# Out rows in two places, nine begun strips, two-bank scores and the Hyena beside five heads in a two-layer hybrid step

## The chip, the cores and the metric

The kernel runs on one NeuronCore of a Trainium2 chip. Five engines work side by side, each through its own queue in order: PE (TensorE, the matrix multiplier), DVE (VectorE), ACT (ScalarE), POOL (GpSimd) and SP (SyncE, which here only starts DMA transfers). They wait for one another through semaphores. Matmul results land in PSUM, which has eight banks of 128 partitions by 512 fp32 numbers; everything else works on SBUF. The metric is the device time of one execution in microseconds, as the median of several.

## What is computed

One inference step of a two-layer backbone on 128 context tokens and 512 latent tokens (T = 640 tokens, D = 1024 channels). Each layer is a half-step SwiGLU, a mixer and a second half-step SwiGLU, each with an RMSNorm before it and a shift, a scale and a gate that depend on the conditioning vector. Layer 0's mixer runs RWKV-7 and a gated DeltaNet side by side, layer 1's runs latent attention (MLA) and an order-2 Hyena convolution. Cut to what the change touches:

```python
def swiglu(x, w_gu, w_down):
    g, u = jnp.split(x @ w_gu, 2, axis=-1)
    return (jax.nn.silu(g) * u) @ w_down          # F = 2816

def pre(x, g, m, j):
    return rmsnorm(x, g) * (1.0 + m[:, :, 3 * j + 1]) + m[:, :, 3 * j]

def rwkv7_mix(p, S0, mu, ...):
    p = p + mu * (centred_shift(p) - p)           # 0.5 * (previous + next token)
    r, k, v, wd, ad, gd = jnp.split(p, A_SPLITS, axis=-1)
    ...

def conv3(p, w):
    prev, nxt = neighbours(p)
    return w[0] * prev + w[1] * p + w[2] * nxt
```

The attention has 8 heads with 64 + 32 query and key channels and 64 value channels. Context tokens see the 128 context tokens, latent tokens see 128 cached tokens and the 512 latent ones, 640 keys, through an ordinary softmax. The Hyena takes 12 projections of 128 channels through conv3 and then two long convolutions, which are done as products with cosine and sine tables.

## The kernel before

Activations lie with channels on partitions: x as two halves (c = 0, 1) of 320 tokens, each 128 x 8 x 320. Products are done to fp32 precision by splitting each operand into a high part and a low part (hh and hl for the normed input, wh and wl for weights) and adding three matmuls. The split of a weight costs an ACT cast (wh) and a subtraction (wl) on DVE or POOL.

**The feed-forwards** (`ffn`, four times: ffn01, ffn02, ffn11, ffn12). The 22 strips of 128 hidden channels stand in five groups (FGROUPS: 5, 4, 4, 4, 5 strips). A strip is a Strassen-Winograd product: seven products of 12 matmuls over quarters of the input, 84 matmuls of 320 columns. Two of the seven need only the first token half. `first(f)` does these two ahead for the strips of group 0 (NE = 5): a *begun strip*, 24 matmuls, whose results wait in the tiles u2 (named u) and s1 (named s). Meanwhile `quarters` makes the sums that the other five products need: r0a and r0b are hi + lo of the first half (L601, on POOL, in the tiles hidh and hidl), then the second half is normed into r1a, r1b, and their differences are split into the tiles b0 to b5 and the second half's hh and hl (L605, on DVE). `strip(f)` then does the remaining products; the sums of weights S come from POOL (L684). After each group the down projection of its hidden strips is added into x (L550). The norm before an ffn is part of the tail of the stage before it (`branch`), so an ffn opens with its begun strips, while the norm of the second half is still being made. With `self.bg` (ffn01 and ffn02 still fetch modulation weights in the background) the strips carry further items beside them; in ffn11 and ffn12 `self.bg` is empty.

**The start.** In block one of the program the Hyena's filters are computed in PSUM banks of two kinds, four "mm" and four "mx". Then `banks(mm=8)` closes that pool and opens eight "mm" banks for ffn01.

**in_proj0** makes 32 rows of projections for layer 0's mixer. Each is a strip of 48 matmuls, copied into a padded tile pp, taken through a token shift (`shift`, 15 rows) or a three-tap convolution (`conv`, 16 rows, four heads of four; one in four only through SiLU) or stored as it is (`gate`) in a tile o, and written to the DRAM tensor pd (320 KB a row), from which the recurrences read it. `shift` adds the neighbours on POOL (nb, L878), scales on ACT (L881) and combines on DVE (L882). `self.t` keeps the number of buffers that was given at a tag's first use in its pool: `shift(0, ...)` comes first and asks for "o" without a number, so that o has one buffer for the whole pool.

**mixers1.** `latents` makes the query, key and value latents. `heads` is a generator over eight heads: `project` makes q and k, `softmax` the scores of 128 queries against 640 keys in two banks of 320, `values` transposes the probabilities pr into PT (L1779) and multiplies by V. `hyena_in` is a generator over the 12 strips of the Hyena's input, `hyena` over its convolutions. Four heads run with three strips each, then four heads with three Hyena steps each.

What sets the order: the code above records instructions in Python order, and the tile framework's scheduler then places them on the engines' queues by a timeline that it models itself, so instructions of neighbouring stages mix. Pools are released tile by tile.

## Time and profile before

| | us |
|---|---|
| three runs | 3175.32, 3182.38, 3186.39 |
| median | 3182.38 |
| the profiled execution | 3187.08 |
| its span | 3185.1 |
| mean granted clock of PE | 0.957 |

The profile is of one execution, with times from the start of its span. A group of the profile stands by its line: L287 is every matmul of the helper `mm`, so tiles tell more than lines there. A busy PE is not a PE at its peak: in the openings of stages the granted clock (1.00 is full speed) drops, and a matmul of 320 columns takes longer. In brackets behind an instruction stands how long its engine sat idle before it and what it was released by; `DMA pd<-o` as a releaser is the writing of a row o to DRAM. Where the stages lie: the filters to about 88 us, ffn01 from there, in_proj0 and the recurrences from 575 to 1303, ffn11 from 1838, the latents of layer 1 up to 2366, heads and Hyena to 2661, ffn12 from 2721.

### The profile page before, as it was taken

To read this page: it belongs to the slowest core of one execution; us is meant where nothing else is said; L and a number is where in the kernel's file an instruction comes from. 1 tells how busy PE (TensorE), PEld (TensorE's weight loads), DVE (VectorE), ACT (ScalarE), POOL (GpSimd) and SP (SyncE) were. 2 spreads that over 40 slices of the span, in tenths; PEclk is the share of its full clock that TensorE was granted. 3 is DMA by queue.
4 is the path that set the end of the run, shared out by engine and by line. 5 is a ranking of instruction groups with operands and counts; after the bars stand their busy time and mean duration, and the time that the engine had idled before them with its cause. 6 is when DMAs were issued, how large, how long until landed. Compare 5 with 4: busy or idle time off the path is not lost.

```text
span 3185.1 us, 56006 instructions
## 1 busy us (share of the span) xinstructions
PE 2958.5 (93%) x21505; PEld 2671.5 (84%) x21505; DVE 2267.1 (71%) x4011; ACT 1355.0 (43%) x2846; POOL 1200.8 (38%) x1114
## 2 busy tenths in 40 slices
PE   7799999998988998889999979999989989899998
PEld 2689999987865676879999979999979748899998
DVE  5956667668769666695666797777766786977777
ACT  3423334566365555442333453333545424433333
POOL 1733335225545220263333474444310021744442
PEclk9999999998888989889999989999999989999999
DMA  7465542455564332445553222222321215222222
GB/s 273 137 209 164 177 137 72 166 157 170 139 151 112 93 86 81 161 146 181 163 180 116 82 93 87 84 86 83 122 62 58 91 47 181 67 90 86 80 83 83
DMA packets 277587, 385.36 MB, mean 121 GB/s; under 512 B 128704, under 2 KB 161120, under 8 KB 275400
## 3 DMA queue, kind: packets, MB, share of 16 engines
q1 hardware_dynamic: 277160, 381.13, 38.3%
q8 instruction: 169, 2.77, 0.4%
q14 instruction: 98, 0.80, 0.1%
q0 software_dynamic: 160, 0.66, 0.0%
HBM read 330.29 MB, written 51.42 MB: 120 GB/s over the span
## 4 chain that ended last, share of the span: by engine, by line
PE 54%; DVE 10%; ACT 4%; DMA 4%; POOL 3%; issue 3%; SPq 1%; DVEq 0%; ACTq 0%; POOLq 0%
PE ps L287 52%; DMA wr<-in_wd_dram 2%; DVE wl L655 1%; POOL S L684 1%; DMA wr<-in_wo_dram 1%; DVE nx L539 1%; DVE wl L471 1%; POOL X L826 0%; POOL wl L655 0%; POOL inv L824 0%; PE ps L1778 0%; DMA pd<-o 0%; DVE nacc L514 0%; DVE b L605 0%; ACT wh L470 0%
## 5 line engine op out<-in xcount | busy, mean ns | idle before, releaser
L287 PE MATMUL ps<-hh,wh 128*128 128x320 f32 x2208 | 698.6, 318 | 17.8 <-DVE g L1901 7.1
L287 PE MATMUL ps<-hl,wh 128*128 128x320 f32 x2208 | 695.1, 316 | 5.4 <-POOL hl L546 2.7
L287 PE MATMUL ps<-hh,wl 128*128 128x320 f32 x2208 | 686.5, 315 | 5.3 <-DVE wl L471 4.2
L287 PE MATMUL ps<-b,wh 128*128 128x320 f32 x2112 | 480.5, 315 | 32.5 <-DVE b L605 17.2
L287 PEld LDWEIGHTS ps<-hh,wh 128*128 128x128 f32 x2208 | 422.4, 192 | 34.4 <-DVE g L1901 7.9
L287 PEld LDWEIGHTS ps<-hl,wh 128*128 128x128 f32 x2208 | 422.8, 192 | 9.7 <-POOL hl L546 3.9
L287 PEld LDWEIGHTS ps<-hh,wl 128*128 128x128 f32 x2208 | 420.3, 191 | 8.8 <-DVE wl L471 5.4
L287 PEld LDWEIGHTS ps<-b,wh 128*128 128x128 f32 x2112 | 360.7, 192 | 40.5 <-DVE b L605 19.4
L287 PE MATMUL ps<-hidl,wh 128*128 128x320 f32 x1248 | 383.7, 309 | 0.0
L287 PE MATMUL ps<-hidh,wh 128*128 128x320 f32 x1248 | 383.2, 312 | 0.0
L287 PE MATMUL ps<-hidh,wl 128*128 128x320 f32 x1248 | 381.7, 309 | 1.0 <-DVE wl L471 1.0
L550 DVE SCALAR_TENSOR_TENSOR x<-ps,mod,x 128x128 f32<-128x128 f32 (+2 forms) x528 | 212.4, 435 | 212.3 <-PE ps L287 211.7
L655 POOL TENSOR_TENSOR wl<-S,wh 128x512 fp32r<-128x512 f32 x176 | 260.5, 1480 | 264.8 <-ACT wh L654 261.6
L684 POOL TENSOR_TENSOR S<-wr,wu 128x512 f32<-128x512 f32 x88 | 125.2, 1423 | 600.9 <-DMA wr<-in_wgu_dram 394.9
L287 PE MATMUL ps<-b,wl 128*128 128x320 f32 x1056 | 330.6, 315 | 9.4 <-DVE wl L655 6.1
L470 ACT CAST wh<-wr 128x512 fp32r<-128x512 f32 (+2 forms) x210 | 157.7, 754 | 407.0 <-PE ps L287 318.0
L654 ACT CAST wh<-S 128x512 fp32r<-128x512 f32 (+1 forms) x264 | 201.0, 763 | 216.0 <-PE ps L287 163.7
L471 DVE TENSOR_TENSOR wl<-wr,wh 128x512 fp32r<-128x512 f32 (+2 forms) x210 | 186.5, 891 | 82.9 <-ACT wh L470 80.9
L287 PEld LDWEIGHTS ps<-hidh,wh 128*128 128x128 f32 x1248 | 232.9, 188 | 13.3 <-issue 7.4
L287 PEld LDWEIGHTS ps<-hidh,wl 128*128 128x128 f32 x1248 | 233.4, 188 | 1.5 <-DVE wl L471 1.5
L287 PEld LDWEIGHTS ps<-hidl,wh 128*128 128x128 f32 x1248 | 234.1, 188 | 0.0
L287 PEld LDWEIGHTS ps<-b,wl 128*128 128x128 f32 x1056 | 202.3, 192 | 13.8 <-DVE wl L655 8.5
(457 smaller groups left out, 5971.2 us busy)
## 6 DMA issues: line engine op xcount, KB each, us to landing
wmod<-in_wmod_dram SPq DMA_DIRECT2D x288, 256.0 KB
wr<-in_wgu_dram SPq DMA_DIRECT2D x108, 512.0 KB
wu<-in_wgu_dram SPq DMA_DIRECT2D x88, 512.0 KB
wr<-in_wd_dram SPq DMA_DIRECT2D x80, 320.0 KB
wr<-in_wd_dram SPq DMA_DIRECT2D x96, 256.0 KB
pd<-o SPq DMA_DIRECT2D x32, 320.0 KB
wr<-in_abg_dram SPq DMA_DIRECT2D x17, 512.0 KB
wr<-in_wo_dram SPq DMA_DIRECT2D x16, 512.0 KB
```

The source lines that it names most:

```text
L287: self.nc.tensor.matmul(out=out, lhsT=lhsT, rhs=rhs, start=start, stop=stop)
L470: nc.scalar.copy(out=wh, in_=w)
L471: nc.vector.tensor_sub(out=wl, in0=w, in1=wh.bitcast(F32))
L539: nc.vector.scalar_tensor_tensor(out=xn[:, a:b], in0=self.x[c][:, k, a:b], scalar=A, in1=r[:, a:b], op0=ALU.mult, op1=ALU.mult)
L550: self.nc.vector.scalar_tensor_tensor(out=self.x[c][:, d, a:b], in0=q[:, a:b], scalar=gate[:, cond, d:d + 1], in1=self.x[c][:, d, a:b], op ...
L654: nc.scalar.copy(out=hi, in_=r)
L655: eng.tensor_tensor(out=lo, in0=r, in1=f32(hi), op=ALU.subtract)
L684: G.tensor_tensor(out=out, in0=x, in1=y, op=op)
```

## The change

Six edits.

1. In `in_proj0` two places for "o" are allocated first in the pool, and every user asks for two. `shift` becomes a `conv3` with weights mu/2, 1 − mu, mu/2: two DVE passes per span in place of POOL's neighbour sum and one DVE pass.
2. `NE` becomes (5, 9): where no background is left (ffn11, ffn12), nine strips are begun, those of groups 0 and 1, and `quarters` is called behind the second begun strip instead of the first.
3. `softmax` takes both score banks as one tile: one reduction, one exponential with one sum, no joining of two maxima and two sums. From head 3 on, PT is copied by ACT.
4. `hyena_in` starts in the latents: one strip behind the query latent, two behind V. Three heads then run beside nine strips, and five heads beside the Hyena, two steps each.
5. The filters' banks stay open: block one goes on with "mm" and "mx" in turn, without closing the PSUM pool.
6. The two part sums of `quarters` (L601) go from POOL to DVE in all four ffns, with the second half's norm sum issued ahead of them.

```diff
--- before.py
+++ after.py
...
-NE = 5
+NE = (5, 9)
...
+NHS = 3
...
     def mm(self, out, lhsT, rhs, start=True, stop=True):
...
-    def ps(self, tag="mm"):
+    def ps(self, tag=None):
+        if tag is None:
+            tag, self.kinds = self.kinds[0], self.kinds[1:] + self.kinds[:1]
...
     def col(self, name, j=0, rows=slice(None)):
...
     def banks(self, **tags):
...
-        self.psum, self.tags = None, tags
+        self.psum, self.tags, self.kinds = None, tags, ["mm"]
...
-    def stat_end(self, c, tag="mm"):
+    def stat_end(self, c, tag=None):
...
-    def finish_norm(self, tag="mm", ks=range(KD), raw=None):
+    def finish_norm(self, tag=None, ks=range(KD), raw=None):
...
+        if self.nr[1] is None:
+            self.stat_end(1)
...
-            nc.gpsimd.tensor_tensor(out=r, in0=hi0[:, k].bitcast(F32), in1=lo0[:, k].bitcast(F32), op=ALU.add)
+            v.tensor_tensor(out=r, in0=hi0[:, k].bitcast(F32), in1=lo0[:, k].bitcast(F32), op=ALU.add)
...
         def split(to, r):
...
-        early = {}
+        early, ne = {}, NE[not self.bg]
...
         def first(f):
...
-            p1, s1 = tile("u2", NE), tile("s1", NE + 1)
+            p1, s1 = tile("u2", ne), tile("s1", ne + 1)
...
-                u, g0 = tile("u2", NE), tile("s1", NE + 1)
+                u, g0 = tile("u2", ne), tile("s1", ne + 1)
...
-                for f in range(NE):
+                for f in range(ne):
...
-                    if f == 0:
+                    if f == (ne > NE[0]):
...
+        out_ = lambda: self.t(ip, [P, T], "o", bufs=2)
+        for _ in range(2):
+            out_()
...
         def gate():
...
-            o = self.t(ip, [P, T], "o", bufs=2)
+            o = out_()
...
         def conv(hh, j):
...
-            o = self.t(ip, [P, T], "o", bufs=2)
+            o = out_()
...
-            nb = self.t(ip, [P, T + 1], "nb")
-            nc.gpsimd.tensor_tensor(out=nb, in0=p[:, 0:T + 1], in1=p[:, 2:T + 3], op=ALU.add)
-            o = self.t(ip, [P, T], "o")
-            for a, b, g in ((0, LP, 0), (LP, T, 1)):
-                nc.scalar.activation(out=o[:, a:b], in_=p[:, a + 1 + g:b + 1 + g], func=AF.Copy, scale=omu[:, mi:mi + 1])
-                nc.vector.scalar_tensor_tensor(out=o[:, a:b], in0=nb[:, a + g:b + g], scalar=hmu[:, mi:mi + 1],
-                                               in1=o[:, a:b], op0=ALU.mult, op1=ALU.add)
+            o = out_()
+            self.conv3(p, (hmu[:, mi:mi + 1], omu[:, mi:mi + 1], hmu[:, mi:mi + 1]), o)
...
-    def latents(self, h, first):
+    def latents(self, h, first, strips):
...
+        next(strips)
...
+        for _ in range(2):
+            next(strips)
...
     def heads(self, ap):
...
         def softmax(hh, qi):
...
-            ss = [self.ps("sc") for _ in keys]
-            mx = self.t(ap, [P, 2], "mxs", bufs=4)
-            sm = self.t(ap, [P, 2], "sms", bufs=4)
-            for i, (k0, n) in enumerate(keys):
-                self.mm(ss[i][:, :n], qt[hh][:96, P * qi:P * qi + P], kt[hh][:96, k0:k0 + n])
-                nc.vector.tensor_reduce(out=mx[:, i:i + 1], in_=ss[i][:, :n], axis=mybir.AxisListType.X, op=ALU.max)
-            if len(keys) > 1:
-                nc.vector.tensor_tensor(out=mx[:, :1], in0=mx[:, :1], in1=mx[:, 1:], op=ALU.max)
-            nc.vector.tensor_scalar(out=mx[:, :1], in0=mx[:, :1], scalar1=-scale, scalar2=None, op0=ALU.mult)
...
+            sc = self.psum.tile([P, 2, 512], F32, tag="sc", name=self.name("ps"), bufs=2)[:, :len(keys)]
+            n = keys[0][1]
+            mx = self.t(ap, [P, 1], "mxs", bufs=4)
+            sm = self.t(ap, [P, 1], "sms", bufs=4)
+            for i, (k0, _) in enumerate(keys):
+                self.mm(sc[:, i, :n], qt[hh][:96, P * qi:P * qi + P], kt[hh][:96, k0:k0 + n])
+            nc.vector.tensor_reduce(out=mx, in_=sc[:, :, :n], axis=mybir.AxisListType.XY, op=ALU.max)
+            nc.vector.tensor_scalar(out=mx, in0=mx, scalar1=-scale, scalar2=None, op0=ALU.mult)
...
-            for i, (k0, n) in enumerate(keys):
-                nc.scalar.activation(out=pr[:, i * H:i * H + n], in_=ss[i][:, :n], func=AF.Exp, scale=scale, bias=mx[:, :1],
-                                     accum_out=sm[:, i:i + 1])
-            if len(keys) > 1:
-                nc.vector.tensor_tensor(out=sm[:, :1], in0=sm[:, :1], in1=sm[:, 1:], op=ALU.add)
-            nc.vector.reciprocal(out=sm[:, :1], in_=sm[:, :1])
-            nc.vector.tensor_scalar(out=pr[:, :nk], in0=pr[:, :nk], scalar1=sm[:, :1], scalar2=None, op0=ALU.mult)
+            nc.scalar.activation(out=pr[:, :nk].rearrange("p (k n) -> p k n", n=n), in_=sc[:, :, :n], func=AF.Exp, scale=scale, bias=mx,
+                                 accum_out=sm)
+            nc.vector.reciprocal(out=sm, in_=sm)
+            nc.vector.tensor_scalar(out=pr[:, :nk], in0=pr[:, :nk], scalar1=sm, scalar2=None, op0=ALU.mult)
...
         def values(hh, qi):
...
-                nc.vector.tensor_copy(out=PT[hh][:, g:g + n, P * (qi - 1):P * qi],
-                                      in_=q[:, :P * n].rearrange("p (k t) -> p k t", k=n))
...
+                (nc.vector.tensor_copy if hh < NHS else nc.scalar.copy)(out=PT[hh][:, g:g + n, P * (qi - 1):P * qi],
+                                                                        in_=q[:, :P * n].rearrange("p (k t) -> p k t", k=n))
...
-                    q = self.ps("tr")
+                    q = self.ps("tr" if "tr" in self.tags else "mx")
...
-        self.banks(mm=8)
+        self.kinds = ["mm", "mx"]
...
-        self.latents(h, first)
...
+        sp = self.pool("strips", bufs=1, reuse_waits="tile")
...
+        strips = self.hyena_in(h, sp)
+        self.latents(h, first, strips)
...
-        sp = self.pool("strips", bufs=1, reuse_waits="tile")
-        heads, strips = self.heads(ap), self.hyena_in(h, sp)
-        for i in range(4):
+        heads = self.heads(ap)
+        for i in range(NHS):
...
-        for i in range(4, 8):
+        for i in range(NHS, 8):
...
-            for _ in range(3):
+            for _ in range(2):
...
```

What the scheduler makes of it, at three places. PE at the start of ffn01: nacc is the sum of squares of the second half, hmi and dfw belong to the last two filter products, and the row with hh, hl and wh is the first begun strip. Before:

```order
L287 MATMUL ps_553<-nacc_530,const_58 128x320
L287 MATMUL ps_499<-hmi_319,dfw_178 128x512 x2
L287 MATMUL ps_500<-hmi_319,dfw_178 128x512 x2
L287 MATMUL ps_647<-hh_581,wh_643 128x320
L287 MATMUL ps_647<-hl_582,wh_643 128x320
L287 MATMUL ps_647<-hh_581,wl_644 128x320
L287 MATMUL ps_647<-hh_581,wh_643 128x320
```

After, from the end of the first begun product on:

```order
L288 MATMUL ps_643<-hh_577,wl_640 128x320
L288 MATMUL ps_731<-hh_577,wh_727 128x320
L288 MATMUL ps_731<-hl_578,wh_727 128x320
L288 MATMUL ps_499<-hmi_319,dfw_178 128x512 x2
L288 MATMUL ps_500<-hmi_319,dfw_178 128x512 x2
L288 MATMUL ps_731<-hh_577,wl_728 128x320
L288 MATMUL ps_659<-hh_577,wh_639 128x320
L288 MATMUL ps_659<-hl_578,wh_639 128x320
```

The first begun product (ps_643) and the start of another strip's now stand ahead of the last two filter products.

DVE where ffn12's quarters are split. L673 is a begun strip's sum s, L655 the split of a weight (wr: of a begun strip), L605 the split pieces, L616 and L617 differences of quarters. Before, the end of that stretch:

```order
L673 TENSOR_TENSOR s_5240_29200<-ps_29202,u_5239_29199 128x320
L605 TENSOR_TENSOR b_5205_29057<-hidh_5200_29052,b_5204_29056 128x1280
L655 TENSOR_TENSOR wl_29274<-S_5256_29261,wh_29273 128x1024
L617 TENSOR_TENSOR hidh_5202_29054<-hidl_5203_29055,hidh_5202_29054 128x1280
L616 TENSOR_TENSOR hidh_5200_29052<-hidl_5203_29055,hidh_5200_29052 128x1280
L673 TENSOR_TENSOR s_5247_29236<-ps_29238,u_5246_29235 128x320
L605 TENSOR_TENSOR b_5207_29059<-hidh_5200_29052,b_5206_29058 128x1280
L605 TENSOR_TENSOR b_5209_29061<-hidh_5202_29054,b_5208_29060 128x1280
L605 TENSOR_TENSOR hl_29070<-hidl_5203_29055,hh_29069 128x1280
L605 TENSOR_TENSOR hl_29070<-hidl_5201_29053,hh_29069 128x1280
```

After (L678, L660, L610, L621 and L622 are the same lines there):

```order
L660 TENSOR_TENSOR wl_29173<-wr_29170,wh_29172 128x1024
L622 TENSOR_TENSOR hidh_5167_28936<-hidl_5168_28937,hidh_5167_28936 128x1280
L678 TENSOR_TENSOR s_5212_29118<-ps_29120,u_5211_29117 128x320
L621 TENSOR_TENSOR hidh_5165_28934<-hidl_5168_28937,hidh_5165_28934 128x1280
L660 TENSOR_TENSOR wl_29209<-wr_29206,wh_29208 128x1024
L678 TENSOR_TENSOR s_5219_29154<-ps_29156,u_5218_29153 128x320
L660 TENSOR_TENSOR wl_29258<-wu_29248,wh_29257 128x512
L610 TENSOR_TENSOR b_5172_28941<-hidh_5165_28934,b_5171_28940 128x1280
L610 TENSOR_TENSOR b_5174_28943<-hidh_5167_28936,b_5173_28942 128x1280
L610 TENSOR_TENSOR hl_28952<-hidl_5168_28937,hh_28951 128x1280
L678 TENSOR_TENSOR s_5226_29190<-ps_29192,u_5225_29189 128x320
```

Between the pieces b and hl now stand sums s of strips 5 to 8 and the splits of their weights wr.

DVE in a head: L1746 and L1755 (after) are the reduction of scores to a maximum, L1748 and L1755 (before) join two maxima and two sums, cv is a Hyena strip's convolution. Before, in an early head:

```order
L1746 TENSOR_REDUCE mxs_25835<-ps_25833 128x1
L1756 RECIPROCAL sms_25765<-sms_25765 128x1
L1748 TENSOR_TENSOR mxs_25810<-mxs_25810 128x1
L1757 TENSOR_SCALAR pr_25769<-pr_25769,sms_25765 128x128
L1749 TENSOR_SCALAR mxs_25810<-mxs_25810 128x1
L1755 TENSOR_TENSOR sms_25811<-sms_25811 128x1
L1756 RECIPROCAL sms_25811<-sms_25811 128x1
L1746 TENSOR_REDUCE mxs_25835<-ps_25834 128x1
L1757 TENSOR_SCALAR pr_25818<-pr_25818,sms_25811 128x640
L1748 TENSOR_TENSOR mxs_25835<-mxs_25835 128x1
L1749 TENSOR_SCALAR mxs_25835<-mxs_25835 128x1
```

After, also beside strips:

```order
L1755 TENSOR_REDUCE mxs_26796<-ps_26795 128x1
L1741 TENSOR_TENSOR q_26766<-ps_26781,rope_25342 32x320
L1742 TENSOR_TENSOR t_26767<-ps_26781,rope_25342 32x320
L1755 TENSOR_REDUCE mxs_26816<-ps_26815 128x1
L1756 TENSOR_SCALAR mxs_26796<-mxs_26796 128x1
L916 SCALAR_TENSOR_TENSOR cv_26752<-pp_4480_25643,cols_59,cv_26752 128x128
L916 SCALAR_TENSOR_TENSOR cv_26752<-pp_4480_25643,cols_59,cv_26752 128x512
L1756 TENSOR_SCALAR mxs_26816<-mxs_26816 128x1
L917 SCALAR_TENSOR_TENSOR cv_26752<-pp_4480_25643,cols_59,cv_26752 128x128
L1760 RECIPROCAL sms_26797<-sms_26797 128x1
L917 SCALAR_TENSOR_TENSOR cv_26752<-pp_4480_25643,cols_59,cv_26752 128x512
L1761 TENSOR_SCALAR pr_26802<-pr_26802,sms_26797 128x640
```

One reduction stands for two, and the two joining rows are gone.

More of the change, by code (lines that the diff above doesn't have):

```diff
@@ L2128, in mixers1 @@
         next(strips, None)
+        self.tc.swap_default_side()
         self.close(sp)
+        self.tc.swap_default_side()
         self.close_w()
```

2 lines of the change are left out of this document (added).

## The prediction

> **What bounds the kernel.** I read the page first: the span, the busy shares and the chain that ended last.
>
> ```profile
> span 3185.1 us, 56006 instructions
> PE 2958.5 (93%) x21505; PEld 2671.5 (84%) x21505; DVE 2267.1 (71%) x4011; ACT 1355.0 (43%) x2846; POOL 1200.8 (38%) x1114
> PE 54%; DVE 10%; ACT 4%; DMA 4%; POOL 3%; issue 3%; SPq 1%; DVEq 0%; ACTq 0%; POOLq 0%
> ```
>
> PE is busy 93% of the span, so 3185.1 − 2958.5 = 226.6 us are idle. Few products are taken out here, so nearly all that the change can win is in those 226.6 us and in the time after an idle stretch in which the granted clock is low. The second reading is therefore stage by stage, at the places that the diff touches: the busy time of each engine in windows. Columns are the stretch, then busy time (instructions) of PE, PEld, DVE, ACT, POOL, then the granted clock. These are the openings of ffn11 (two rows) and ffn12 (four rows).
>
> ```profile
> 1837.80:1849.30 11.50, 2.88 (x16) 1.88 (x14) 11.39 (x14) 7.47 (x17) 9.38 (x10) 0.74 0.39 141
> 1849.30:1891.00 41.70, 31.34 (x170) 28.95 (x171) 38.42 (x32) 21.70 (x33) 32.51 (x15) 0.83 0.26 86
> ...
> 2720.80:2739.40 18.60, 18.43 (x124) 17.87 (x122) 17.11 (x14) 11.30 (x19) 16.00 (x7) 1.00 0.36 121
> 2739.40:2763.30 23.90, 14.69 (x61) 13.05 (x62) 22.84 (x20) 11.80 (x18) 20.43 (x8) 0.79 0.18 60
> 2763.30:2804.50 41.20, 37.47 (x241) 35.10 (x240) 40.41 (x49) 14.87 (x27) 28.67 (x20) 1.00 0.24 81
> 2804.50:2880.00 75.50, 75.50 (x517) 75.50 (x516) 51.03 (x81) 25.87 (x43) 32.99 (x23) 1.00 0.29 88
> ```
>
> The five begun strips run at full rate (18.43 of 18.60). Then the quarters have to be made, and PE works 14.69 of 23.90 at a granted clock of 0.79 while DVE is 96% busy; until 2804.5 DVE is the bound (40.41 of 41.20). From there PE is. In ffn11 the hole is 11.50 − 2.88 = 8.6 us, then 10.4 us in the next row.
>
> **Nine begun strips (ffn11, ffn12).** The 124 matmuls of the first ffn12 row take 18.6 us, 0.150 each; a begun strip is 24 of them, 3.6 us, so four more are 14.4 us of PE per ffn that go ahead of the wait and no longer stand in group 1, where PE is the bound. If all of it fell into idle time each ffn would win 14.4. It will not, because DVE is full there. Prices of what the four strips and the part sums put on DVE:
>
> ```profile
> 2744.41 1.22 DVE L655 TENSOR_TENSOR wl<-S,wh 128x1024 fp32r<-128x1024 f32 x1
> 2745.55 1.48 DVE L617 TENSOR_TENSOR hidh<-hidl,hidh 128x1280 f32<-128x1280 f32 x1
> ...
> 2748.35 0.48 DVE L673 TENSOR_TENSOR s<-ps,u 128x320 f32<-128x320 f32 x1
> ```
>
> Four splits of 1.22, four sums of 0.48 and two part sums of 1.48 make 4.9 + 1.9 + 3.0 = 9.8 us. In ffn12 some 2 us fall into what DVE leaves free before 2739.4 and 2804.5 (1.5 + 1.1 + 0.8 = 3.4), and POOL, without its sums, stretches DVE less; I let group 0 end 6 us later. Group 1 (the last row begins with the products of group 0 and goes on with it) has room on DVE, 51.03 of 75.50, and each of its four begun strips needs 3.6 us less of PE, of which I count 2.75, as DVE can't quite keep that pace: −11. Net −5 in ffn12. ffn11 has the larger hole (8.6 + 10.4 = 19 us of idle PE in its rows against 0.2 + 9.2 + 3.7 = 13 in ffn12's first three), so −6. Bounds: −14.4 each if the holes swallow everything, +8 if DVE's 9.8 stretch further and group 1 gives back little. The four more weight loads of 512 KB lie where the DMA share is 0.36 or less.
>
> **Part sums on DVE (all four ffns).** Two adds leave POOL for DVE. What POOL's adds do to DVE is visible at the start of ffn01:
>
> ```profile
> 88.93 2.87 POOL L601 TENSOR_TENSOR hidl<-hh,hl 128x1280 f32<-128x1280 f32 x1
> ...
> 88.99 3.16 DVE L539 SCALAR_TENSOR_TENSOR nsq<-x,A,nacc 128x320 f32<-128x320 f32 x1
> 92.08 0.54 DVE L539 SCALAR_TENSOR_TENSOR nx<-x,A,nacc 128x320 f32<-128x320 f32 x1
> ```
>
> The same DVE form takes 3.16 beside the add and 0.54 just after. So one POOL add can cost DVE 2.6 us, and on DVE it costs 1.48. In ffn11 and ffn12 this is in the sum above. In ffn01 and ffn02 nothing else changes on DVE: I take −1 for both together, bounds −4 (the 2.6 saved twice, 1.48 paid twice, in each) and +6 (2.96 paid in each, nothing saved). [...]
>
> **The filters' PSUM banks kept in block one.** Before, ffn01's first product waits for the last bank of the filters.
>
> ```profile
> 94.06 0.68 DVE L1901 SCALAR_TENSOR_TENSOR g<-fa,ps 128x512 f32<-128x512 f32 x1
> ...
> 94.79 0.64 PE L287 MATMUL ps<-hh,wh 128*128 128x320 f32 x1 [7.09 <-DVE g L1901]
> 95.23 0.47 PE L287 MATMUL ps<-hl,wh 128*128 128x320 f32 x1
> ...
> 98.96 0.35 PE L287 MATMUL ps<-hh,wh 128*128 128x320 f32 x1
> ```
>
> That is 7.1 us of idle, and then 15 matmuls until 98.96 that take 4.2 us instead of 15 × 0.15 = 2.3: two more. Both can go, 9 us at most. But the work behind the begun strips waits for the quarters, whose DVE chain doesn't hang on these banks, so most of the 9 us will reappear as a wait for the pieces b. I count −3, bounds −9 and +3 (the products issued ahead delay the filters' own last ones, and with them the bank that DVE empties).
>
> **Out rows in two places (in_proj0).** The row "o" had one buffer, and each strip's activation waited until the row before was written out.
>
> ```profile
> L878 POOL TENSOR_TENSOR nb<-pp 128x641 f32<-128x641 f32 x15 | 27.3, 1818 | 65.5 <-issue 33.7 <-ACT pp L751 26.1 <-DVE o L882 5.6
> L882 DVE SCALAR_TENSOR_TENSOR o<-nb,hmu,o 128x512 f32<-128x512 f32 x15 | 13.1, 876 | 0.6 <-ACT o L881 0.6
> L913 DVE SCALAR_TENSOR_TENSOR o<-pp,cols,o 128x512 f32<-128x512 f32 x12 | 9.0, 754 | 0.2
> ...
>   DMA pd<-o: 65.6, 22
> ...
> 830.71 1.02 ACT L911 ACTIVATE o<-pp,cols 128x128 f32<-128x128 f32 x2 [11.93 <-DMA pd<-o]
> 898.49 0.77 ACT L864 ACTIVATE o<-ps 128x320 f32<-128x320 f32 x2 [3.27 <-DMA pd<-o]
> 899.72 2.50 PE L287 MATMUL ps<-wd,lora 128*128 128x320 f32 x4 [9.05 <-ACT w L1051]
> ...
> 775.00:825.00 50.00, 44.35 (x310) 41.03 (x311) 36.79 (x71) 18.82 (x43) 35.55 (x70) 0.83 0.60 155
> 825.00:875.00 50.00, 43.80 (x476) 42.31 (x475) 38.97 (x75) 17.38 (x36) 26.67 (x44) 0.86 0.46 140
> 875.00:925.00 50.00, 35.68 (x202) 27.25 (x200) 30.38 (x39) 27.34 (x69) 28.45 (x59) 0.83 0.55 143
> ```
>
> Engines stood 65.6 us, in 22 waits, for the write of o (tile view of o). Behind a waiting ACT queue the weight casts and the biases of the recurrence, and at 899.7 PE has been idle 9.05 us for one of them. PE's idle time in the three windows is 26.2 us, the clock another 150 − (0.83 + 0.86 + 0.83) × 50 = 24; together 50 us is the ceiling. Against it, DVE gets a second pass per span: 15 × (0.754 + about 0.35, the 128x128 form being about half) = 16.5 us, while POOL loses 27.3. SP's queue keeps its order of blocked writes and weight loads, so some of the waits stay. I take somewhat under a quarter of the 50: −11; bounds −26 (all the idle time) and +16 (DVE's second passes on the path, no wait gone).
>
> **Two-bank scores and the Hyena beside five heads.**
>
> ```profile
> 2375.00:2525.00 150.00, 149.71 (x952) 134.54 (x951) 103.70 (x262) 72.94 (x200) 11.96 (x9) 1.00 0.16 49
> 2525.00:2630.00 105.00, 89.91 (x314) 49.96 (x313) 94.53 (x203) 24.66 (x74) 24.40 (x17) 0.92 0.24 83
> 2630.00:2661.00 31.00, 24.40 (x121) 17.22 (x119) 16.90 (x45) 8.42 (x24) 4.13 (x4) 0.97 0.36 125
> ...
> L1746 DVE TENSOR_REDUCE mxs<-ps 128x1 f32<-128x320 f32 x64 | 30.2, 484 | 3.9 <-PE ps L287 3.6
> L1779 DVE COPY PT<-ps 128x512 f32<-128x512 f32 x32 | 21.9, 686 | 8.9 <-PE ps L1778 8.8
> L1779 DVE COPY PT<-ps 128x128 f32<-128x128 f32 x32 | 9.1, 284 | 2.5 <-PE ps L1778 2.5
> L1755 DVE TENSOR_TENSOR sms<-sms 128x1 f32<-128x1 f32 x32 | 8.7, 273 | 9.8 <-ACT pr L1752 9.4
> L1748 DVE TENSOR_TENSOR mxs<-mxs 128x1 f32<-128x1 f32 x32 | 7.6, 239 | 0.2
> ...
> L1752 ACT ACTIVATE pr<-ps,mxs 128x320 f32<-128x320 f32 x64 | 33.2, 525 | 40.3 <-PE ps L1778 28.1 <-DVE mxs L1749 12.2
> L1752 ACT ACTIVATION_READ_ACCUMULATOR pr<-ps,mxs 128x1 f32 x72 | 14.3, 198 | 0.0
> ```
>
> While strips run beside the heads PE is full; while the Hyena does, DVE is (94.53 of 105) and PE idles 15.1 and runs at 0.92. The change takes from DVE 8.7 + 7.6, about 5 on the reduction (the 512-wide copy costs 0.402 more than the 128-wide, 1.05 ns a column, so a 640-wide reduction is about 0.484 + 0.335 = 0.82 against 0.97 for two; bounds 0.5 and 1.0), and five eighths of the PT copies, 19.4: some 40 us. ACT gets the 19.4, loses about 8 of exponentials and 32 × 0.198 = 6.3 of reads, and has the room (24.66 of 105). The Hyena now has five heads to hide behind instead of four, and three of its strips lie ahead, in the latents. Ceiling: idle 0.3 + 15.1 + 6.6 and clock 0.08 × 105 + 0.03 × 31 = 9.3, some 31 us. The last softmax, its values and the mix rows keep most of the 6.6; some of the rest stays between dependent steps: −20, bounds −31 and −3 (the steps of a softmax, which follow on one another, set the pace and not DVE's sum).
>
> **Sum.** −5 − 6 − 1 − 3 − 11 − 20 = −46 on the profiled execution's 3187.1 (its span and 2.0 around it), 3141. That execution was 4.7 us above the median of the three, so on the median the forecast is 3136.4.
>
> **Rivals.**
> - Everything idle is used: both ffns near −14, in_proj0 −20, the mixer −28, the filters −7: −83 on the median, 3099, with 3090 to 3118 around it. For it speaks that every named wait stands in the profile beside work that is ready; against it that DVE is the next engine in each place. 0.18.
> - Half of it only: PE already full beside the strips (149.71 of 150) makes the mixer −8, and SP's queue keeps o's writes late, so in_proj0 is 0. Then −5 − 6 − 1 − 3 − 8 = −23, 3159, with 3150 to 3173. 0.26.
> - No difference: the recurrences behind in_proj0 are a chain of small steps whose order changes with it; if they give back what the projections win, and DVE holds both ffns at 0, some −4 is left: 3178. 0.09.
> - Slower, by DVE alone: its new work is 2 × 9.8 in ffn11 and ffn12, 2 × 3.0 in ffn01 and ffn02, 16.5 in in_proj0, 42 us in all, and in ffn11, ffn12 and in_proj0 it is 71 to 98% busy by the windows above. Beside POOL its forms double (the 3.16 against 0.54 is the extreme), and then the 42 become 84; less 22 won in group 1 and 20 in the mixer that is +42 on the path if all lies there, 3224, and about 3195 if two thirds do. It decides from the point where more than 42 us of those 84 lie on the path. Against it: in in_proj0 DVE has 44 of 150 us free. 0.08.
>
> **How the numbers follow.** The forecast, 3118 to 3150, has 0.39, the rivals 0.18, 0.26, 0.09 and 0.08. A measurement of this kernel can tell about 0.3%, 9.5 us, from no change. Faster by more is 0.39 + 0.18 + 0.26 = 0.83; within it 0.09; slower 0.08. The range leaves out the lower half of the first rival, the slower one and the last part of no difference, less than 0.2 in all: 3097 to 3181.
>
> **What would show it.** In the profile after: PE at the start of ffn01 without a wait for L1901's bank, and whether a longer wait for b takes its place. Nine begun strips ahead of strip 0 in ffn11 and ffn12, an idle PE of less than 4 us between them and it, a group 0 that ends some 6 us later and a group 1 about 11 us shorter. In in_proj0 waits for the write of o below 30 us in sum, and PE above 0.90 in clock. From the first head to the end of the mixer DVE busy for 175 us or less instead of 215, and PE idle for less than 12 instead of 22. I am wrong if the openings of ffn11 and ffn12 get longer by more than 10 us with DVE full, if the first strips in the latents hold up q and V, or if the recurrences' stretch, which I count at nothing, moves by more than 10.

## The result, and the profile after

The changed kernel takes 3130.66 us (median of 4 runs, 3126.78 to 3135.70) against 3183.58 (4 runs) before: a ratio of 0.9839, with an interval of 0.9815 to 0.9863, or 53 us. The forecast was 3136.4 and the range 3097 to 3181. The whole came out as forecast; the terms did not, and the study is about these.

The page of the changed kernel, with the lines that answer to those of before (span, busy shares):

```profile
span 3126.9 us, 55884 instructions
PE 2934.4 (94%) x21505; PEld 2653.1 (85%) x21505; DVE 2231.4 (71%) x3913; ACT 1365.5 (44%) x2825; POOL 1157.1 (37%) x1091
```

PE idles 192.5 us instead of 226.6, and its busy time, in which slow-clock matmuls count longer (in the recurrences, with one order of instructions, 263.71 us at a clock of 0.92 and 280.17 at 0.86, below), fell by 24.1: 58 us of span in this pair of profiles. Where it lies is found by marks: the starts of the same matmuls in both traces (the last product of a down projection, the last one that reads lora, the first and last that read kh, which is the out projection's weight). The row of ffn12 goes to the end of the last matmul. Differences of these marks, in us, for before and for two profiles of the changed kernel, the second from another session:

| stretch | before | after | after, again | forecast of the change |
|---|---|---|---|---|
| start and ffn01, to its last down product | 578.1 | 576.9 | 576.2 | −3.5 |
| in_proj0, to the last lora product | 387.5 | 378.2 | 379.9 | −11 |
| recurrences, to the first kh product | 312.4 | 295.9 | 294.9 | 0 |
| out projection and ffn02, to its last strip | 518.6 | 516.6 | 522.1 | −0.5 |
| ffn11, to its last down product | 499.4 | 487.1 | 486.7 | −6 |
| latents, heads, Hyena, to the last kh product | 424.5 | 417.7 | 416.3 | −20 |
| ffn12, to its last matmul | 454.9 | 445.1 | 445.0 | −5 |

The openings of the two ffns with nine begun strips show it best. Windows of the changed kernel, columns as before (ffn11's opening and its group 0, then ffn12's begun strips, the wait, the rest of group 0, and as long a piece of group 1 as before):

```profile
1814.00:1847.50 33.50, 29.17 (x180) 27.99 (x181) 32.59 (x35) 26.52 (x46) 11.18 (x5) 0.95 0.35 110
1847.50:1902.20 54.70, 48.84 (x322) 46.95 (x321) 49.10 (x59) 20.65 (x36) 48.49 (x29) 1.00 0.30 100
...
2672.30:2704.00 31.70, 31.70 (x217) 31.54 (x216) 28.58 (x32) 26.12 (x41) 4.70 (x3) 1.00 0.32 106
2704.00:2719.00 15.00, 9.77 (x48) 8.91 (x48) 12.57 (x9) 4.28 (x7) 15.00 (x7) 0.77 0.18 59
2719.00:2760.80 41.80, 39.66 (x261) 37.98 (x260) 40.15 (x50) 16.95 (x30) 34.52 (x23) 1.00 0.28 92
2760.80:2836.30 75.50, 74.49 (x509) 74.22 (x508) 53.24 (x87) 22.60 (x38) 35.28 (x24) 1.00 0.31 96
```

The nine begun strips run without a gap (31.70 of 31.70), the wait behind them leaves 5.2 us of idle PE where it left 9.2, and in the last row PE is all but full (74.49 of 75.50), with DVE at 53 of 75. From its first down product to its last, ffn12 is 14.4 us shorter than before: group 1 gives back what the four strips took.

The place of the filters' banks: PE in ffn01's opening (in brackets the idle time and its releaser).

```profile
106.60 0.52 PE L288 MATMUL ps<-hh,wl 128*128 128x320 f32 x1 [3.86 <-DVE wl L660]
116.40 0.41 PE L288 MATMUL ps<-b,wh 128*128 128x320 f32 x1 [3.45 <-ACT b L609]
```

The wait of 7.09 us for a bank is gone, and the first begun strip starts at 84.1 us instead of 94.8. In place of that wait PE now waits 3.86 for a weight's split and 3.45 for the second of the three pieces b that ACT casts. And the tile view of o, the waits for the write of a row:

```profile
  DMA pd<-o: 14.7, 5
```

They fell from 65.6 us in 22 waits to 14.7 in 5.

### The profile page after: what moved, and what is told of

Same layout as the page of the kernel before. It is cut to its first block, busy times and chain, and to the rows that moved or that the text cites. A ratio compares the mean times of both kernels' runs of the same rounds, so it can differ in the third digit from the quotient of the medians.

```text
span 3126.9 us, 55884 instructions
## 1 busy us (share of the span) xinstructions
PE 2934.4 (94%) x21505; PEld 2653.1 (85%) x21505; DVE 2231.4 (71%) x3913; ACT 1365.5 (44%) x2825; POOL 1157.1 (37%) x1091
## 4 chain that ended last, share of the span: by engine, by line
PE 48%; DVE 8%; DMA 3%; ACT 2%; issue 2%; POOL 2%; SPq 0%; DVEq 0%; ACTq 0%; POOLq 0%
PE ps L288 47%; DMA wr<-in_wd_dram 1%; DVE wl L660 1%; POOL S L689 1%; DMA wr<-in_wo_dram 1%; POOL wl L660 0%; DVE nx L542 0%; PE ps L1782 0%; DVE nacc L517 0%; DVE wl L474 0%; DVE hidl L479 0%; DMA wr<-in_wgu_dram 0%; DVE x L553 0%; DVE mxs L1755 0%; DVE nacc L509 0%
## 5 line engine op out<-in xcount | busy, mean ns | idle before, releaser
L288 PEld LDWEIGHTS ps<-hh,wl 128*128 128x128 f32 x2208 | 419.0, 191 | 19.2 <-DVE wl L660 9.5
L689 POOL TENSOR_TENSOR S<-wr,wu 128x512 f32<-128x512 f32 x88 | 132.2, 1503 | 615.3 <-DMA wr<-in_wgu_dram 450.9
L660 POOL TENSOR_TENSOR wl<-S,wh 128x512 fp32r<-128x512 f32 x176 | 256.6, 1458 | 230.8 <-ACT wh L659 230.0
L474 DVE TENSOR_TENSOR wl<-wr,wh 128x512 fp32r<-128x512 f32 (+2 forms) x210 | 184.6, 881 | 84.1 <-ACT wh L473 80.5
```

The lines of the kernel that those rows point to most:

```text
L288: self.nc.tensor.matmul(out=out, lhsT=lhsT, rhs=rhs, start=start, stop=stop)
L474: nc.vector.tensor_sub(out=wl, in0=w, in1=wh.bitcast(F32))
L660: eng.tensor_tensor(out=lo, in0=r, in1=f32(hi), op=ALU.subtract)
L689: G.tensor_tensor(out=out, in0=x, in1=y, op=op)
```

## The experiments

All twelve were compared with the kernel before on their own chip. Nine take the changed kernel and undo or alter one part; one puts a single part into the kernel before; one is the changed kernel itself, once more; one repeats the kernel with new banks. Marks as above; "the changed kernel" there means the mean of its two profiles.

How far profiles differ where the code is the same has to stand beside each of these differences. Six profiles that have the changed kernel's order of instructions to the end of the recurrences show 575.6 to 579.8 us for the start with ffn01, 378.1 to 380.6 for in_proj0 and 294.0 to 311.7 for the recurrences. Nine with the changed mixer show 412.6 to 417.7 for latents, heads and Hyena together. The total swings with the recurrences, and only three of the other eleven (new banks the second time, POOL's sum with two places, the rows alone) ran on one chip with the changed kernel's repeat, so a part is judged by its stretch first.

### Rows

One place for o:

```diff
-        out_ = lambda: self.t(ip, [P, T], "o", bufs=2)
-        for _ in range(2):
-            out_()
+        out_ = lambda: self.t(ip, [P, T], "o", bufs=1)
+        out_()
```

> The changed kernel with one place for o instead of two (shift stays a conv3). The stage between ffn01's last product and the out projection took 26 us less after the change than before. Theory, waits on the write of o: the second place brings most of it, so the stage grows by 18 us or more and the total goes to about 3150 us. Rival, the conv3 form (POOL relieved of 15 sums): the stage grows by less than 8, total 3131 to 3138. Rival, order: the scheduler's new order of the recurrences made the gain, then the part before the recurrences (to the last lora product) moves by less than 5 and only the rest changes.

3167.73 us, ratio 0.9965 (0.9953 to 0.9977). in_proj0 takes 389.6, 10.6 longer; the recurrences 314.4, 19 longer. The tile view of o in that kernel:

```profile
  DMA pd<-o: 53.3, 18
```

The waits are back, and with them more time than in_proj0 had won. The part in in_proj0 holds the theory, though with 10.6 us and not the 18 that it asked of the whole stretch; the 19 us behind it, and a total 18 us above the 3150 of the theory, are taken up below.

One place, and POOL's neighbour sum (the first edit and):

```diff
-            self.conv3(p, (hmu[:, mi:mi + 1], omu[:, mi:mi + 1], hmu[:, mi:mi + 1]), o)
+            nb = self.t(ip, [P, T + 1], "nb")
+            nc.gpsimd.tensor_tensor(out=nb, in0=p[:, 0:T + 1], in1=p[:, 2:T + 3], op=ALU.add)
+            ...
```

> The changed kernel with in_proj0 as before (one place for o, POOL's neighbour sum in shift). Theory, waits on the write of o: within 5 us of the kernel with one place and conv3, total 3150 to 3157. Rival, the conv3 form: 15 us or more above that kernel. If DVE's second passes cost something, this kernel is below it by up to 8.

3157.15 us, ratio 0.9940 (0.9925 to 0.9955): 10.6 below the kernel with one place and conv3, a little more than allowed for. But in_proj0 is 386.4, only 3.2 shorter; the rest lies in stretches that this edit doesn't touch. With one place, DVE's second passes cost about 3 us, little more than the 2.5 by which equal kernels differ there.

Two places, and POOL's sum made per span so that it fits:

```diff
+            nb = self.t(ip, [P, T - LP], "nb")
+            for a, b, g in ((0, LP, 0), (LP, T, 1)):
+                nc.gpsimd.tensor_tensor(out=nb[:, :b - a], in0=p[:, a + g:b + g], in1=p[:, a + 2 + g:b + 2 + g], op=ALU.add)
+                ...
```

> The changed kernel with two places for o but POOL's neighbour sum in shift (made per span, so that it fits beside the second place). One place instead of two cost 13 us in in_proj0, and with one place POOL's form was 3.6 us faster than conv3. Theory: the two add up, in_proj0 (first to last lora product) takes 283 to 287 us against 288 to 290, and the total is 0 to 6 us below the changed kernel's. Rival, with two places the DVE passes are hidden: in_proj0 within 2 us of the changed kernel's. Rival, POOL is late in that stretch: longer by 3 or more.

3145.97 us, ratio 0.9894 (0.9870 to 0.9917), 13.3 above the changed kernel on the same chip. From the first to the last lora product 294.5, against 291.1 in the repeat that ran beside it (287.8 to 291.1 in all six profiles of that order): longer by 3.4 or more, as the last rival had it; most of the other 10 us are in the recurrences (306.8). So conv3 loses a little with one place and wins a little with two; that POOL is late is what the rival says, and it was not tested by itself, since the scheduler gives each of these kernels another order there. No better kernel came of it.

The rows alone, in the kernel before (in_proj0 as changed, nothing else):

> The kernel before with the changed in_proj0 alone (two places for o, conv3). Theory: in_proj0 wins 8 to 12 us as it does in the changed kernel, and the recurrences behind it between 0 and 17, total 3155 to 3172 where before has 3176 to 3183. Rival, the gain needs the other edits: within 5 us of before.

3175.16 us against 3181.70, ratio 0.9983 (0.9969 to 0.9998), −6.5: neither the theory's 3155 to 3172 nor quite the rival. in_proj0 is 383.2, 4.3 shorter than before, about half of what it wins in the changed kernel. Its waits for the write of o are 16.7 us, so they went as fully. What the other half needs can be read from a run below: from ffn01's end to the end of the recurrences this kernel has the order of instructions of the changed kernel with new banks, but for two DVE instructions, and that one takes 383.0 and 383.8 in in_proj0 in its two profiles. So the other 4 us or so come with the order that the scheduler finds when the filters' banks are kept.

### Begun strips and part sums

Five begun strips everywhere:

```diff
-NE = (5, 9)
+NE = (5, 5)
```

> The changed kernel with five begun strips in all four ffns and quarters behind the first (part sums stay on DVE). After the change ffn11 with its opening was 12 us shorter than before, ffn12 10. Theory, begun strips fill the idle openings: 8 to 12 us come back in each, total 3147 to 3155. Rival, the part sums on DVE did it: less than 3 in each, total 3131 to 3137. Rival, DVE is full in the openings and the strips brought nothing: 3131 or below.

3152.31 us, ratio 0.9919 (0.9904 to 0.9935). ffn11 takes 496.2, 9.3 longer; ffn12 451.8, 6.8 longer: the theory, at or just under its lower bound. Most of what the two ffns won is the begun strips (with the place of `quarters`, which this edit moves back too). The two kernels differ in both pieces of ffn12: the nine begun strips make the opening 6.0 us longer (88.6 against 82.6) and the stretch from the first to the last down product 12.8 shorter (353.4 against 366.2). Windows of that kernel in ffn12 (begun strips, wait, rest of group 0):

```profile
2690.90:2710.90 20.00, 18.92 (x126) 18.09 (x124) 17.23 (x17) 13.27 (x20) 7.09 (x6) 1.00 0.34 118
2710.90:2735.00 24.10, 13.67 (x51) 12.09 (x51) 20.20 (x20) 11.39 (x18) 18.54 (x8) 0.68 0.15 56
2735.00:2773.40 38.40, 37.48 (x251) 37.22 (x251) 34.99 (x46) 16.39 (x28) 29.21 (x20) 0.98 0.27 87
```

The hole is there again: 10.4 us idle, at a clock of 0.68.

Part sums on POOL:

```diff
-            v.tensor_tensor(out=r, in0=hi0[:, k].bitcast(F32), in1=lo0[:, k].bitcast(F32), op=ALU.add)
+            nc.gpsimd.tensor_tensor(out=r, in0=hi0[:, k].bitcast(F32), in1=lo0[:, k].bitcast(F32), op=ALU.add)
```

> The changed kernel with the two part sums of quarters on POOL again. Theory: each POOL add holds DVE up for more than its own price there, so each ffn loses 1 to 3 us, total 3134 to 3142. Rival, the sums were the main gain in ffn11 and ffn12: 5 to 10 in each, total 3141 to 3151. Rival, DVE full: moving them back wins, total 3120 to 3128.

3138.88 us, ratio 0.9874 (0.9840 to 0.9908). Its four runs go from 3125.9 to 3147.4, so the total says nothing here. ffn11 492.7, 5.8 longer (the other kernels with nine begun strips have 486.6 to 490.0); ffn12 445.4 and ffn02 519.2, the same; the stretch to ffn01's end 574.9, 1.6 shorter, which is less than equal kernels differ there. The sums on DVE win in one ffn of four; in the others nothing is shown either way.

### The filters' banks

```diff
-        self.kinds = ["mm", "mx"]
+        self.banks(mm=8)
```

> The changed kernel with the filters' PSUM banks closed and eight new ones opened before ffn01. Theory: the first begun product waits for the filters' last bank again and comes 7 to 9 us later, but the work behind the begun strips waits for the quarters anyway, so ffn01 ends 1 to 4 us later, total 3132 to 3137 where the changed kernel has 3127 to 3131. Rival, the opening was on the path: 7 to 9 us later at ffn01's end. Rival, nothing: within 1.

3147.86 us, ratio 0.9910 (0.9895 to 0.9925). The first begun strip starts 8 us later and the first product with a piece b 5.5 us later than in the changed kernel's profiles (108.3 against 102.4 and 103.3), but ffn01 ends at 572.7, 3.9 *earlier*. None of the three expectations; the total is yet higher.

Why ffn01 ends earlier is in the traces. The pieces b themselves come earlier with new banks: ACT casts the three of them at 96.2, 104.9 and 106.6 us, in the changed kernel at 99.9, 115.1 and 116.2. There the second cast waits 3.16 us for DVE's difference L621, which starts at 112.50 behind the sums s and splits wl of the begun strips that the kept banks let go ahead. Windows from 100 to 130 us, of the changed kernel and of this one:

```profile
100.00:115.00 15.00, 9.08 (x50) 8.56 (x48) 15.00 (x13) 7.24 (x14) 10.68 (x7) 0.89 0.62 226
115.00:130.00 15.00, 11.68 (x49) 10.71 (x50) 13.94 (x12) 7.40 (x8) 11.61 (x6) 0.66 0.10 35
...
100.00:115.00 15.00, 13.42 (x90) 12.88 (x88) 14.94 (x10) 11.59 (x20) 10.81 (x5) 1.00 0.40 136
115.00:130.00 15.00, 10.77 (x52) 10.06 (x53) 11.07 (x10) 5.00 (x8) 13.84 (x8) 0.77 0.32 104
```

With the kept banks PE idles 9.2 us there instead of 5.8, and at a lower clock (0.89 and 0.66 against 1.00 and 0.77); it does 99 matmuls where it does 142 with new ones. Because this kernel had run beside other kernels only, it ran again beside the changed kernel:

> The changed kernel once more, unaltered. Five of the kernels run so far have its very order of instructions up to the recurrences' end, and their profiles show 294 to 312 us between the last lora product and the first out projection, with a granted clock of 0.93 to 0.86 there. Theory, the clock in that stretch differs from one execution to the next: this profile shows 290 to 315 us there, stage time less the part of it that the clock withheld is 267 to 274 again, and its runs spread over 8 us or more. Rival, the 296 of the first profile is a property of this kernel: 294 to 298, and all other stages within 1.

> The kernel with new PSUM banks before ffn01 once more, beside the changed kernel on the same chip. Its profile had ffn01's end 4 us earlier than the changed kernel, but its runs were 15 us and more above it. Theory, the recurrences' clock and their other order made that: beside the changed kernel on one chip the medians differ by less than 10 us and ffn01 ends 3 to 5 us earlier again. Rival, keeping the banks is worth 15 us or more: the difference of medians stays there.

The changed kernel: 3132.66 us (3130.37 to 3142.86), ratio 0.9863 (0.9839 to 0.9887). With new banks: 3147.68, ratio 0.9895 (0.9873 to 0.9917); the medians differ by 15.0, the rival's bound, the means of these five and six runs by 10, and ffn01 ends at 574.0, 2.2 earlier. The difference isn't in the opening: in_proj0 takes 383.9 against 379.9, and the recurrences 311.3 against 294.9. Those two stretches have another order of instructions in this kernel. The 4 us of in_proj0 are clear of the spread; the recurrences' are not, as shown below.

### Scores, PT and the fifth head

Softmax as before (two reductions, two exponentials, joined):

```diff
-            nc.vector.tensor_reduce(out=mx, in_=sc[:, :, :n], axis=mybir.AxisListType.XY, op=ALU.max)
+                nc.vector.tensor_reduce(out=mx[:, i:i + 1], in_=ss[i][:, :n], axis=mybir.AxisListType.X, op=ALU.max)
+            if len(keys) > 1:
+                nc.vector.tensor_tensor(out=mx[:, :1], in0=mx[:, :1], in1=mx[:, 1:], op=ALU.max)
...
```

> The changed kernel with softmax as before: two reductions, two exponentials, joined maxima and sums (PT still on ACT from head 3). The mixer with latents won only 7 us, where 20 were forecast. Theory A, DVE relief is what counts: the mixer grows by 10 or more, total 3138 to 3150. Theory B, a softmax's steps follow on one another and the fewer steps count: the heads beside the Hyena grow by 5 to 10, the heads beside strips by less than 2. Rival, neither: less than 3 in all.

3141.30 us, ratio 0.9891 (0.9874 to 0.9908). Latents, heads and Hyena together take 425.0, 8.0 longer. All of it lies beside the Hyena (9.3, below); beside the strips nothing is lost (117.9 us from the first query product to the first dfp one, against 118.7). These are theory B's numbers. But DVE also has more to do, so this run doesn't tell fewer steps from less DVE work.

PT on DVE for all heads:

```diff
-                (nc.vector.tensor_copy if hh < NHS else nc.scalar.copy)(out=PT[hh][:, g:g + n, P * (qi - 1):P * qi],
+                nc.vector.tensor_copy(out=PT[hh][:, g:g + n, P * (qi - 1):P * qi],
```

> The changed kernel with PT copied by DVE in all heads. It puts 19 us back on DVE, which is busy for 96 of 120 us beside the Hyena after the change. Theory A, DVE is still the bound there: the mixer grows by 8 to 19. Theory B, chains bound it: less than 4 either way.

3149.25 us, ratio 0.9918 (0.9901 to 0.9934). The stretch takes 422.1, 5.1 longer, between the two theories; much of the rest of its time is in the recurrences (304.1). Here the number of steps is the same, so what it loses beside the Hyena (7.6, below) goes with DVE's load and not with the length of the chain.

Strips and heads as before (mixers1 of before, no strip in the latents):

> The changed kernel with no strip in the latents, twelve strips beside four heads and the Hyena beside four, as before (two-bank scores and PT on ACT from head 3 kept). Theory, the strips moved into the latents cost their full time there and the Hyena beside five heads idles PE as before: the mixer with its latents ends within 4 us of the changed kernel's, the stretch beside the Hyena keeps its 14 us of idle PE. Rival, the fifth head fills the Hyena's idle time: it ends 8 to 15 later. Rival, the move costs: it ends 4 or more earlier, and the best kernel is this one.

3135.37 us, ratio 0.9885 (0.9859 to 0.9911). The stretch takes 419.0, 2.0 longer: the theory, and not clear of the 412.6 to 417.7 that kernels with the changed mixer show. Nor does the total tell the two kernels apart. The windows of the Hyena alone, from its first product with dfp to its last with div, in the changed kernel, with the old softmax, with PT on DVE and with four heads:

```profile
2466.10:2597.30 131.20, 117.34 (x459) 71.27 (x458) 99.77 (x188) 42.14 (x107) 32.69 (x22) 0.96 0.22 74
```

```profile
2467.50:2608.00 140.50, 125.27 (x463) 74.52 (x462) 108.15 (x244) 45.93 (x141) 30.96 (x22) 0.91 0.21 71
```

```profile
2480.00:2618.80 138.80, 122.39 (x464) 73.20 (x463) 110.75 (x225) 29.56 (x73) 32.38 (x22) 0.94 0.21 71
```

```profile
2510.50:2623.90 113.40, 103.01 (x386) 62.12 (x385) 88.22 (x166) 33.73 (x86) 29.81 (x19) 0.95 0.24 82
```

Beside the Hyena the joined scores are worth 9.3 us and PT on ACT 7.6, both clear of noise: the nine profiles with the changed mixer have 130.3 to 131.7 us there, at a clock of 0.96 or 0.97. DVE's busy time in these windows falls by 8.4 and 11.0 us (108.15 and 110.75 to 99.77); for all 20 softmaxes of five heads the rows would give 20 × (2 × 0.484 − 0.820 + 0.239 + 0.273) = 13 us and 19, but three of them lie outside. Little of the gain is idle time of PE, which falls by 1.4 and 2.6 only; the rest is PE busy for 7.9 and 5.0 us less with nearly the same matmuls, at a clock of 0.96 in place of 0.91 and 0.94. A fifth head there costs 131.2 − 113.4 = 17.8. It wins 40 us in the stretch before, with its three strips (158.7 from the first query product to the first dfp one with four heads and twelve strips, 118.7 with three and nine), but the strips cost 17.4 in the latents (92.4 against 75.0). 40 − 17.8 − 17.4 leaves 5, of which the tail behind the last div product takes back 3 (74.9 against 71.8; the nine profiles have 70.5 to 74.9 there).

### The recurrences

Six of these kernels have one and the same order of instructions on every engine up to the recurrences' end: the changed kernel, its repeat, and those with five begun strips, the old softmax, PT on DVE and four heads. Their profiles differ there all the same. Windows from the last lora to the first kh product, of the changed kernel, the old softmax, PT on DVE and four heads (the granted clock stands third from the end):

```profile
955.00:1250.90 295.90, 263.71 (x3246) 194.26 (x3244) 213.94 (x650) 164.16 (x556) 85.30 (x178) 0.92 0.36 96
```

```profile
958.10:1252.10 294.00, 262.23 (x3246) 192.42 (x3244) 215.40 (x650) 164.15 (x556) 85.18 (x178) 0.93 0.36 96
```

```profile
959.10:1263.20 304.10, 273.61 (x3245) 200.49 (x3244) 214.68 (x650) 164.10 (x556) 85.07 (x178) 0.88 0.35 93
```

```profile
956.10:1267.80 311.70, 280.17 (x3245) 205.51 (x3244) 214.28 (x650) 164.11 (x556) 85.17 (x178) 0.86 0.33 91
```

DVE, ACT and POOL work the same to a per cent, and PE's idle time is 30.5 to 32.2 us in all four; its busy time is not the same. Length times clock gives 272, 273, 268 and 268. By these figures the stretch is as long as the granted clock makes it, and with the same order of instructions its length differs from one execution to the next by up to 18 us. The kernel with new banks fits too:

```profile
957.80:1269.10 311.30, 271.95 (x3200) 201.82 (x3198) 212.59 (x645) 167.52 (x553) 81.11 (x175) 0.87 0.34 92
```

311.3 × 0.87 = 271. So does before, in the profile that the forecast was worked from:

```profile
965.50:1277.90 312.40, 277.03 (x3265) 205.28 (x3264) 217.86 (x650) 165.94 (x560) 82.87 (x178) 0.87 0.34 91
```

312.4 × 0.87 = 272. The kernel with one place for o had 314.4 at 0.87, which is 274, so its 19 us need no more than a clock that before had too. Runs of one kernel spread accordingly: before from 3172 to 3192 us, four heads from 3134 to 3152, and the profile of the latter is that of its longest run. The repeat of the changed kernel had 294.9 at 0.92, which its rival named as well; that rival falls by the other stretches (5.5 us in the one with ffn02) and by the five kernels of the same order.

## Why the prediction was right, and where its terms were not

- **The sum** had 46 us where 53 were measured (3136.4 us against 3130.66), by terms that erred both ways: ffn11 and ffn12 won 22 instead of 11, the mixer 7 instead of 20, and a stretch that was set at nothing shows 17 in the profiles. That these errors cancelled is luck. Without the recurrences this pair of profiles differs by 41 us. How much of the 17 belongs to the change stays open: over the sessions the 37 runs of before go from 3172.0 to 3192.0 us and the nine of the changed kernel from 3126.8 to 3142.9, and the profiled execution of before, 3187.08, is longer than all but one of these 37.
- **Nine begun strips.** The mechanism was right, an idle opening filled and a PE-bound group shortened. The mis-sized term is "of which I count 2.75, as DVE can't quite keep that pace": ffn12 from its first down product to its last is 14.4 us shorter than before (367.9 to 353.5), 3.6 for each of four strips, and 12.8, or 3.2 each, against the kernel with five begun strips; in ffn11 the figures are 12.7 and 12.7. DVE has 22 of 75 us to spare there. The opening of ffn12 got 4.6 longer (84.0 to 88.6) where 6 was counted, and 6.0 against five begun strips; ffn11's only 0.4 to 1.1. The idle PE behind the begun strips, expected below 4 us, is 5.2. That DVE is full in the openings (busy 28.58 of 31.70 us, 12.57 of 15.00 and 40.15 of 41.80 in ffn12's begun strips, wait and rest of group 0) did not turn the gain, so the slower rival's mechanism is there at its small price only.
- **Part sums.** The −1 in ffn01 and ffn02 can't be told from nothing: undoing them changed the one by −1.6 and the other by 0, within the spread. Inside ffn11 they bring 3 to 6 us, which the sum had no term of its own for; in ffn12 nothing.
- **Banks kept.** The term has the wrong sign for ffn01. The bank's wait went, as forecast, and PE waits later instead. But the premise that failed is that the quarters' "DVE chain doesn't hang on these banks": with the kept banks it comes later, ACT's second and third casts of b by 8 to 10 us, behind the begun strips' own DVE work. ffn01 ends 2 to 4 us later with the kept banks, where −3 was forecast. The prediction named such a price only for the filters' last products. The whole kernel is yet faster with them on one chip, by 15 us in the medians, through the order and the clock of stretches that the edit doesn't touch: about 4 us in in_proj0, and in the recurrences an amount that their clock hides.
- **Rows.** Waits for the write of o were forecast below 30 us and are 14.7; in_proj0 won 8 to 9 us where 11 was forecast. Undoing the second place costs 10.6 there. The gain is not the row's alone: put into the kernel before it is 4.3, and the rest comes with the order that goes with the kept banks.
- **Scores and the fifth head.** This term fell short, 7 for 20. What failed is the step that DVE's relief of 40 us and the fifth head would empty the 31 us of idle and slow PE. The relief came: from the first query product to the first kh product DVE is busy 37 us less. But PE idles 20.9 us there where it idled 22.0 (less than 12 was expected), and its clock is 0.97 where it was 0.96. Before and after:

```profile
2372.20:2661.10 288.90, 266.86 (x1393) 204.56 (x1393) 215.31 (x510) 107.51 (x301) 40.49 (x29) 0.96 0.21 70
2347.40:2611.80 264.40, 243.54 (x1234) 180.72 (x1234) 178.04 (x360) 103.22 (x254) 41.60 (x29) 0.97 0.21 70
```

  Nearly all of the 24.5 us by which this stretch is shorter is PE's own work, and most of that went into the latents. Relief on DVE pays beside the Hyena only (9.3 and 7.6 us for 8.4 and 11.0 of DVE's busy time); in the stretch with strips PE is full (118.02 of 118.70 us), and it pays nothing (117.9 us with the old softmax), as the rival "half of it only" had it. And moving strips and a head moves PE's work: the latents took the three strips at 17.4 us, the Hyena the head at 17.8, so the move itself brought about 2, which the spread doesn't tell from nothing. The reduction was sized rightly, as the group of the changed kernel shows:

```profile
L1755 DVE TENSOR_REDUCE mxs<-ps 128x1 f32<-128x640 f32 x32 | 26.2, 820 | 4.1 <-PE ps L288 3.9
```

- **The recurrences** "which I count at nothing" moved by 17 in the profiles, beyond the 10 that the prediction named as its own failure. At 0.92 against 0.87 the clock accounts for all of it (272 in both). Whether the new order makes a higher clock more frequent stays open: with the changed kernel's order the six profiles have 0.93, 0.92, 0.92, 0.90, 0.88 and 0.86, and with the part sums on POOL, where that stretch has the same order, 0.88; with one place for o 0.87 and 0.88, with new banks 0.90 and 0.87, with the rows alone 0.90.
- **A reading.** The slower rival takes DVE as "71 to 98% busy" in ffn11, ffn12 and in_proj0; the windows shown go from 61% (30.38 of 50.00) to 99% (11.39 of 11.50). Its "Beside POOL its forms double" was the author's estimate, and the traces show no one factor. In ffn12's wait before, DVE had

```profile
2743.02 1.48 DVE L605 TENSOR_TENSOR b<-hidh,b 128x1280 fp32r<-128x1280 f32 x1
...
2749.76 4.87 DVE L605 TENSOR_TENSOR b<-hidh,b 128x1280 fp32r<-128x1280 f32 x2 [0.92 <-ACT b L604]
2754.55 6.71 DVE L605 TENSOR_TENSOR hl<-hidl,hh 128x1280 fp32r<-128x1280 f32 x2
```

  and POOL was busy with one form from 2744.19 to 2749.57 and from there almost without a gap. From 2749.76 on a form of 128x1280 took 2.44 and 3.36 us on average, 1.6 and 2.3 times the 1.48; the split of 1.22 at 2744.41 and the difference of 1.48 at 2745.55, in the prediction's rows, took no longer while POOL's form of 5.38 lasted.

## What to carry to other kernels

Work moved into an idle opening pays most of its price back where the stage that it leaves is bound by the same engine: here 3.2 to 3.6 us of 3.6 a strip, less what the opening grows by. Moved from one full stretch into another it paid 2 us of 40, whatever it freed elsewhere, so read both ends in windows before moving it. A relief of an engine has to be priced in the stretch where it acts: DVE's was worth about its own size beside the Hyena (9.3 and 7.6 us for 8.4 and 11.0) and nothing beside the strips, where PE was full (118.02 of 118.70 us), and much of its worth showed as less busy time of PE (7.9 and 5.0 us) at a higher granted clock (0.96 against 0.91 and 0.94) and not as less idle time (1.4 and 2.6 us). Starting a stage's first work earlier can make the stage end later, when that work goes ahead of what its later part waits for, as the kept banks did in ffn01, which ended 2 to 4 us later. And before a gain of one per cent is put down to an edit, look for a stretch whose clock differs between executions of the same order: here the recurrences, at 0.86 to 0.93, swing by up to 18 us, more than most of the six edits are worth.

## What the hardware showed that was not expected

The granted clock in the recurrences came out between 0.86 and 0.93 for one order of instructions, with PE idle for 30.5 to 32.2 us in the four windows of that order shown, and the stretch took 294 to 312 us. What sets it from one execution to the next is not shown by any run here.

The other is how long DVE's and POOL's forms last beside each other in ffn12's opening after the change (start, length):

```profile
2705.47 4.15 POOL L623 TENSOR_TENSOR hidl<-hidl,hidh 128x1280 f32<-128x1280 f32 x1
```

```profile
2693.20 1.47 DVE L610 TENSOR_TENSOR b<-hidh,b 128x1280 fp32r<-128x1280 f32 x1
...
2701.78 5.08 DVE L610 TENSOR_TENSOR b<-hidh,b 128x1280 fp32r<-128x1280 f32 x2
2706.79 4.19 DVE L610 TENSOR_TENSOR hl<-hidl,hh 128x1280 fp32r<-128x1280 f32 x1
```

A DVE form of that size takes 1.47 while POOL rests (the first DVE row; POOL starts again at 2699.30); here it starts 1.32 behind POOL's form, ends 1.36 behind it, and lasts 4.19. What is left of it behind POOL's end is close to the 1.47 that such a form takes alone, so the 2.83 before that may be waiting; the rows give no more than start and length. POOL's form looks the same from the other side: it starts while DVE's pair of forms b still runs, ends 2.76 behind that pair's end (2706.86) and lasts 4.15, and a form of this size took it 2.87 at the start of ffn01 before the change. By these rows both queues lose, DVE 2.72 us and POOL 1.28. Whether moving what POOL still does there would save more than moving DVE's own work was not tried.
